# The first product of the second MLP in seven half products a pair of tiles, in place of eight

## The chip, the cores and the metric

The program runs on one core of a Trainium2 chip. The metric is the device time of one execution in microseconds (us). Before the change the median of three runs was 1889.66 us (1889.51 to 1891.02). The profile is of one execution; its span, from the first to the last instruction, is 1887.1 us.

## The reference, cut to what matters

The reference is one inference step of a two-layer diffusion backbone over 128 context tokens and 512 latent tokens, 640 in all, each of 1024 features. Each layer is a mixer (attention in layer 0, retention in layer 1) and an MLP of 4096 intermediate features with a squared ReLU:

```python
h = _rms(x, norm_mlp) * (1.0 + sc2) + sh2
x = x + g2 * (jnp.square(jax.nn.relu(h @ mlp_w1)) @ mlp_w2)
```

With h of 640 x 1024, `mlp_w1` of 1024 x 4096 and `mlp_w2` of 4096 x 1024, the two products of an MLP have the same number of multiplications. The change concerns `h @ mlp_w1` of layer 1, the last MLP before the final norm.

## The kernel before

Activations stand by feature: `xT` and the modulated input `ha` are tiles of 128 features x 640 tokens, and the 640 tokens are two halves of 320. Every number in a product is kept as a high part (fp32r, made by a cast on ScalarE, ACT) and a low part (what the cast left, made by a subtraction on VectorE, DVE). `mm` (L420 to L424) forms high x high, high x low and low x high: three matmuls for each contraction tile of 128 and each half of the tokens. In `ha` contraction tiles 0 to 7 are high parts and 8 to 15 low parts.

The MLP makes its 4096 intermediate features in 32 tiles of 128 (`w1(n)`), in four chunks of 8 tiles. A tile costs 8 contraction tiles x 2 halves x 3 = 48 matmuls of 128x320. `hidden` takes it out of PSUM: ReLU (L1217), square (L1218) and the cast (L841) on ACT, and the low part (L842) on DVE, into `g`. After each chunk 8 tiles of the second product (`w2`, also 48 matmuls each) read the chunk in `g`, and `residual` (L457, DVE) adds them to `xT`. For chunks 1 to 3 the first tile of the next chunk is multiplied before the `w2` tiles (`ahead`), and its ReLU comes after them.

Weights are streamed in one fixed order, `PLAN`: parts of 128x1024 numbers, two parts (1 MB) to a DMA into a buffer `wr`, of which there are two. `pump` prepares a part: the cast into `wh` (L180, ACT), and later, in `lows`, the subtraction into `wl` (L193, DVE). Four prepared parts are held (`SLOTS`); `done()` frees one after a tile and prepares the next. The instructions of each engine run in the order in which this code issues them. Sums of products stand in four PSUM tiles of two banks (`pp`), used in turn.

## Time and profile before

| | |
|---|---|
| median of three runs | 1889.66 us |
| profiled execution, span | 1887.1 us |
| PE (TensorE matmul) busy | 1825.5 us, 97% |
| DVE (VectorE) busy | 1074.8 us, 57% |
| ACT (ScalarE) busy | 782.0 us, 41% |
| POOL (GpSimd) busy | 185.0 us, 10% |
| HBM traffic | 94 GB/s over the span |

Only the medians and spans are given: of the profiled execution no other time than its span is known, so 2.56 us stand between it and the median. The second MLP runs from about 1413 us to the end. "Busy" of PE is from modelled ends of pipelined matmuls, so how close PE is to its rate is read from the starts of its matmuls. In a row of the timeline the first column is the start in us from the span's start, the second the duration in us; in brackets stands the idle time before it and who ended it.

### The profile page before, as it was taken

To read this page: it belongs to the slowest core of one execution; us is meant where nothing else is said; L and a number is where in the kernel's file an instruction comes from. 1 tells how busy PE (TensorE), PEld (TensorE's weight loads), DVE (VectorE), ACT (ScalarE), POOL (GpSimd) and SP (SyncE) were. 2 spreads that over 40 slices of the span, in tenths; PEclk is the share of its full clock that TensorE was granted. 3 is DMA by queue.
4 is the path that set the end of the run, shared out by engine and by line. 5 is a ranking of instruction groups with operands and counts; after the bars stand their busy time and mean duration, and the time that the engine had idled before them with its cause. 6 is when DMAs were issued, how large, how long until landed. Compare 5 with 4: busy or idle time off the path is not lost.

```text
span 1887.1 us, 28520 instructions
## 1 busy us (share of the span) xinstructions
PE 1825.5 (97%) x11844; PEld 1715.8 (91%) x11844; DVE 1074.8 (57%) x1855; ACT 782.0 (41%) x1288; POOL 185.0 (10%) x242
## 2 busy tenths in 40 slices
PE   6998899999999999999999999999999999999997
PEld 4885688999999999998898898899899999999997
DVE  5767887668778663466645645555556332323235
ACT  5546776561322413266324324324347224142332
POOL 0124754200000000030000000000011000000002
PEclk9999999999999999999999999999999999999999
DMA  8205201135544432222122122112112222122111
GB/s 325 95 26 201 90 23 33 58 143 197 196 157 167 149 133 67 68 79 68 66 90 67 68 86 71 68 67 71 65 66 85 73 69 88 67 72 86 68 67 57
DMA packets 44481, 179.01 MB, mean 95 GB/s; under 512 B 3232, under 2 KB 5536, under 8 KB 40768
## 3 DMA queue, kind: packets, MB, share of 16 engines
q1 hardware_dynamic: 42624, 171.81, 26.3%
q0 software_dynamic: 1728, 5.38, 0.8%
q8 instruction: 93, 1.52, 0.3%
q14 instruction: 36, 0.29, 0.0%
HBM read 170.10 MB, written 7.08 MB: 94 GB/s over the span
## 4 chain that ended last, share of the span: by engine, by line
PE 89%; DVE 6%; ACT 2%; issue 1%; POOL 1%; DMA 0%; SPq 0%; POOLq 0%; DVEq 0%; ACTq 0%
PE pp L420 25%; PE pp L422 25%; PE pp L424 25%; PE pp L1433 2%; PE pp L1435 2%; PE pp L1434 2%; PE pt L891 1%; DVE ha L408 1%; PE s L837 1%; DVE xT L457 1%; PE s L838 1%; POOL p L1014 1%; PE x L260 1%; PE pv L898 1%; DVE tl L1029 1%
## 5 line engine op out<-in xcount | busy, mean ns | idle before, releaser
L180 ACT CAST wh<-wr 128x1024 fp32r<-128x1024 f32 x212 | 221.7, 1049 | 729.6 <-PE pp L422 706.5
L422 PE MATMUL pp<-ha,wh 128*128 128x320 f32 x1728 | 410.6, 310 | 7.3 <-DVE ha L408 7.2
L420 PE MATMUL pp<-ha,wh 128*128 128x320 f32 x1728 | 415.4, 312 | 0.0
L424 PE MATMUL pp<-ha,wl 128*128 128x320 f32 x1728 | 409.4, 309 | 1.7 <-DVE wl L193 1.7
L422 PEld LDWEIGHTS pp<-ha,wh 128*128 128x128 f32 x1728 | 292.8, 188 | 11.3 <-DVE ha L408 11.1
L420 PEld LDWEIGHTS pp<-ha,wh 128*128 128x128 f32 x1728 | 292.6, 188 | 8.0 <-issue 5.6
L424 PEld LDWEIGHTS pp<-ha,wl 128*128 128x128 f32 x1728 | 292.8, 188 | 2.3 <-DVE wl L193 2.0
L193 DVE TENSOR_TENSOR wl<-wr,wh 128x1024 fp32r<-128x1024 f32 x212 | 258.1, 1219 | 34.1 <-ACT wh L180 33.2
L457 DVE SCALAR_TENSOR_TENSOR xT<-pp,mod,xT 128x128 f32<-128x128 f32 (+1 forms) x360 | 135.6, 433 | 229.3 <-PE pp L424 229.3
L420 PE MATMUL pp<-g,wh 128*128 128x320 f32 x1024 | 245.4, 310 | 0.0
L422 PE MATMUL pp<-g,wh 128*128 128x320 f32 x1024 | 243.3, 308 | 0.0
L424 PE MATMUL pp<-g,wl 128*128 128x320 f32 x1024 | 243.3, 308 | 0.0
L420 PEld LDWEIGHTS pp<-g,wh 128*128 128x128 f32 x1024 | 173.2, 188 | 3.5 <-issue 3.3
L422 PEld LDWEIGHTS pp<-g,wh 128*128 128x128 f32 x1024 | 173.9, 188 | 0.2
L424 PEld LDWEIGHTS pp<-g,wl 128*128 128x128 f32 x1024 | 173.7, 188 | 0.0
L842 DVE TENSOR_TENSOR g<-s,g 128x640 fp32r<-128x640 f32 x64 | 52.8, 825 | 194.5 <-ACT g L841 194.5
L370 POOL TENSOR_TENSOR acc<-acc,sq 128x320 f32<-128x320 f32 x55 | 52.7, 959 | 995.8 <-ACT sq L366 993.5
L295 DVE SCALAR_TENSOR_TENSOR acc<-la,scond,acc 128x512 f32<-128x512 f32 x196 | 134.4, 746 | 0.0
L420 PE MATMUL pp<-qk,wh 128*128 128x320 f32 (+1 forms) x320 | 88.9, 326 | 0.0
L422 PE MATMUL pp<-qk,wh 128*128 128x320 f32 (+1 forms) x320 | 88.7, 326 | 0.0
L424 PE MATMUL pp<-qk,wl 128*128 128x320 f32 (+1 forms) x320 | 88.7, 325 | 0.0
L1014 POOL TENSOR_TENSOR p<-p,den 128x640 f32<-128x640 f32 (+2 forms) x64 | 70.0, 1095 | 51.2 <-DVE den L1007 25.7
(277 smaller groups left out, 2542.8 us busy)
## 6 DMA issues: line engine op xcount, KB each, us to landing
wr<-in_w SPq DMA_DIRECT2D x121, 1024.0 KB, 4.9
la<-in_wl SPq DMA_DIRECT2D x28, 1024.0 KB, 4.8
raw<-in_w SPq DMA_DIRECT2D x8, 1024.0 KB, 15.8
out_st<-o POOLq DMA_DIRECT2D x16, 256.0 KB, 2.6
xT<-in_x SPq DMA_DIRECT2D x4, 640.0 KB, 6.0
out_y<-xT SPq DMA_DIRECT2D x6, 320.0 KB, 2.3
wr<-in_w SPq DMA_DIRECT2D x2, 512.0 KB, 16.3
con<-in_con SPq DMA_DIRECT2D x1, 640.0 KB, 16.8
```

Source lines behind the costliest of these rows:

```text
L180: nc.scalar.copy(hi, r)
L193: self.nc.vector.tensor_tensor(lo, r, hi.bitcast(F32), ALU.subtract)
L295: nc.vector.scalar_tensor_tensor(a, w, s, a, ALU.mult, ALU.add)
L370: nc.gpsimd.tensor_tensor(acc, acc, sq[:, :HALF], ALU.add)
L420: mm(out[i], wh, rh[i], start=start, stop=False)
L422: mm(out[i], wh, rl[i], start=False, stop=False)
L424: mm(out[i], wl, rh[i], start=False, stop=stop)
L457: self.nc.vector.scalar_tensor_tensor(x, ps[:, s - o:e - o], g[:, k:k + 1], x, ALU.mult, ALU.add)
L842: self.nc.vector.tensor_tensor(lo, src, hi.bitcast(F32), ALU.subtract)
L1014: nc.gpsimd.tensor_tensor(p, p, d.to_broadcast(p.shape), ALU.mult)
L1433: mm(out, self.ha[:, kt, q], hi[:, c], start=kt == 0, stop=False)
L1434: mm(out, self.ha[:, kt, q], lo[:, c], start=False, stop=False)
```

## The change

`PAIRED = (1,)` sends the MLP of layer 1 to `mlp_paired`. Tiles 0 to 7 are made as before. Tiles 8 to 31 are made as 12 pairs by `pair_products`, four pairs in each of three chunks. For a pair the weights are four quarters of 128x512, q0 and q1 (the first tile's two halves of the contraction), q2 and q3 (the second tile's), all in one buffer `wr`. The input is four quarters H(i,j), with token half i and contraction half j. A product of a weight quarter and an input quarter is 4 contraction tiles x 3 = 12 matmuls of 128x320. There are seven, named here by the part of the weights and the form of the input:

- a/11 = q0 H(0,0) and a/12 = q1 H(0,1); c/1 = (q2-q0) S1; c/3 = (q3-q2) S3; d/2 = (q3-q2+q0) S2; d/22 = (q1-(q3-q2+q0)) H(1,1); b/4 = q3 S4
- S1 = H(1,0)+H(1,1), S2 = S1-H(0,0), S3 = H(0,0)-H(1,0), S4 = H(0,1)-S2

Three PSUM tiles take them: `a` gathers a/11, d/2, c/3 and d/22 one after the other, `b` c/1 and b/4, `cc` a/12. Between, ACT copies `a` out three times (into x0, y0, y1), and DVE adds `cc` and `b`. `forms` makes the S in 8 steps, beside tiles 5 to 7 and the first five `w2` tiles; S3 takes the place of H(1,0) in `ha`. `sums_ahead` and `more_sums` make the sums of the weights, the second in place in `wr`. The parts a, c and d of a pair use the four slots; b has a room of its own (`ph`, `pl`, one buffer each), is prepared by `last_part`, and only then is `wr` given back for the next DMA. `old` holds a pair's last steps and runs in the next pair, behind its d/2. The tile made `ahead` is gone. The diff, without its hunks that only take out comments:

```diff
     def mlp(l):
         m = [("w1", l, n) for n in range(8)]
+        if l in PAIRED:
+            for c in range(3):
+                m += [("w2", l, c, n) for n in range(8)]
+                m += [("w1", l, 8 * (c + 1) + n) for n in range(8)]
+            return m + [("w2o", l, r, n) for r in (6, 7) for n in range(4)]
         for c in range(4):
...
     def fill(self):
-        done = self.pos - bool(self.low) - self.pending
+        done = self.behind[0][0] if self.behind else self.pos - bool(self.low) - self.pending
         while self.dma_at < self.most and self.dma_at < (done // 2 + RAWS) * 2:
...
                 return
+            elif paired(what):
+                if self.held >= SLOTS:
+                    return
+                self.pair_part(raw, what)
             else:
                 if self.held >= SLOTS:
...
+    def sums_ahead(self):
+        if self.sub == 0 and self.sums is None and paired(PLAN[self.pos]):
+            q = self.raws[self.pos // 2].rearrange("p (q n) -> p q n", q=4)
+            self.sums = self.pairs.tile([P, SUB + SUB // 4], F32, tag="sums", name="sums")
+            t = self.sums[:, :SUB].rearrange("p (q n) -> p q n", q=2)
+            self.nc.vector.tensor_tensor(t, q[:, 2:4], q[:, 0:3:2], ALU.subtract)
+    def more_sums(self):
+        if self.sub == 1 and not self.summed:
+            self.lows()
+            q = self.raws[self.pos // 2].rearrange("p (q n) -> p q n", q=4)
+            t = self.sums[:, SUB // 2:SUB]
+            self.nc.vector.tensor_tensor(q[:, 0], t, q[:, 0], ALU.add)
+            self.nc.vector.tensor_tensor(q[:, 1], q[:, 1], q[:, 0], ALU.subtract)
+            self.summed = True
+    def pair_part(self, raw, what):
+        k = self.sub
+        if k == 0:
+            self.sums_ahead()
+        elif k == 1:
+            self.more_sums()
+        hi = self.wsp.tile([P, SUB], F32R, tag="wh", name="wh")
+        lo = self.wsp.tile([P, SUB], F32R, tag="wl", name="wl")
+        self.held += 1
+        src = self.sums[:, :SUB] if k == 1 else raw[:, :SUB]
+        self.nc.scalar.copy(hi, src)
+        self.lows()
+        self.low = (lo, src, hi)
+        self.parts[what[1], what[2] // 2, "acd"[k]] = hi, lo
+        self.sub = (k + 1) % 3
+        if k == 1:
+            self.summed = False
+        if k == 2:
+            self.sums = None
+            self.behind.append((self.pos, (what[1], what[2] // 2, "b"), raw))
+            self.pos += 2
+    def last_part(self):
+        self.lows()
+        i, key, raw = self.behind.pop(0)
+        hi = self.pairs.tile([P, SUB // 2], F32R, tag="ph", name="ph")
+        lo = self.pairs.tile([P, SUB // 2], F32R, tag="pl", name="pl")
+        src = raw[:, 3 * SUB // 2:]
+        self.nc.scalar.copy(hi, src)
+        self.nc.vector.tensor_tensor(lo, src, hi.bitcast(F32), ALU.subtract)
+        self.parts[key] = hi, lo
+        self.fill()
+    def part(self, *what):
+        while what not in self.parts:
+            self.pump()
+        return self.parts[what]
...
+    def forms(self, sf):
+        nc = self.nc
+        tt = nc.vector.tensor_tensor
+        def quarter(i, j, lo, k):
+            kt = 8 * lo + 4 * j + k
+            return self.ha[:, kt:kt + 2, HALF * i:HALF * i + HALF].bitcast(F32)
+        def split(hi, lo, t):
+            nc.scalar.copy(hi, t)
+            tt(lo, t, hi.bitcast(F32), ALU.subtract)
+        for k in (0, 2):
+            a, b = (self.tmp.tile([P, NT], F32, tag="t", name=n).rearrange("p (k n) -> p k n", k=2) for n in "ab")
+            out = [[sf[:, f, i, k:k + 2] for i in range(2)] for f in range(3)]
+            tt(a, quarter(1, 0, 0, k), quarter(1, 1, 0, k), ALU.add)
+            tt(b, quarter(1, 0, 1, k), quarter(1, 1, 1, k), ALU.add)
+            tt(a, a, b, ALU.add)
+            split(*out[0], a)
+            yield
+            tt(a, a, quarter(0, 0, 0, k), ALU.subtract)
+            tt(a, a, quarter(0, 0, 1, k), ALU.subtract)
+            split(*out[1], a)
+            yield
+            tt(a, quarter(0, 1, 0, k), a, ALU.subtract)
+            tt(a, a, quarter(0, 1, 1, k), ALU.add)
+            split(*out[2], a)
+            yield
+            tt(a, quarter(0, 0, 0, k), quarter(1, 0, 0, k), ALU.subtract)
+            tt(b, quarter(0, 0, 1, k), quarter(1, 0, 1, k), ALU.subtract)
+            tt(a, a, b, ALU.add)
+            split(*(self.ha[:, k + 8 * i:k + 2 + 8 * i, HALF:] for i in range(2)), a)
+            yield
+    def pair_products(self, l, c, sf, g):
+        nc = self.nc
+        st = {}
+        def form(f):
+            if f in ("1", "2", "4"):
+                return [sf[:, "124".index(f), i] for i in range(2)]
+            i, j = {"11": (0, 0), "12": (0, 1), "22": (1, 1), "3": (1, 0)}[f]
+            return [self.ha[:, 8 * o + 4 * j:8 * o + 4 * j + 4, HALF * i:HALF * i + HALF] for o in range(2)]
+        def product(p, w, half, f, out, start, stop, ks=range(4)):
+            hi, lo = self.part(l, p, w)
+            ah, al = form(f)
+            for k in ks:
+                s = slice(512 * half + P * k, 512 * half + P * k + P)
+                self.mm([out], hi[:, s], lo[:, s], [ah[:, k]], [al[:, k]], start and k == 0, stop and k == ks[-1],
+                        more=not start)
+        def begin(p):
+            a = self.pp()[:, :HALF]
+            x, y = (self.tmp.tile([P, NT], F32, tag="t", name=n) for n in "xy")
+            st[p] = a, x, y
+            product(p, "a", 0, "11", a, True, True)
+            nc.scalar.copy(x[:, :HALF], a)
+        def free():
+            self.held -= 1
+        first = 4 * (c + 1)
+        self.last_part()
+        old = None
+        for p in range(first, first + 4):
+            end = p == first + 3
+            if p == first:
+                begin(p)
+            a, x, y = st.pop(p)
+            b = self.pp()[:, :HALF]
+            x0, x1, y0, y1 = (t[:, HALF * i:HALF * i + HALF] for t in (x, y) for i in range(2))
+            product(p, "c", 0, "1", b, True, True)
+            product(p, "d", 0, "2", a, False, True)
+            if old:
+                old()
+            self.more_sums()
+            nc.scalar.copy(y0, a)
+            cc = self.pp()[:, :HALF]
+            product(p, "a", 1, "12", cc, True, True, range(2) if end else range(4))
+            if not end:
+                free()
+                nc.vector.tensor_tensor(x0, cc, x0, ALU.add)
+                self.pump()
+                nc.scalar.activation(x0, x0, ACTF.Relu)
+                self.lows()
+            product(p, "c", 1, "3", a, False, True)
+            free()
+            nc.scalar.copy(y1, a)
+            nc.vector.tensor_tensor(y1, b, y1, ALU.add)
+            self.pump()
+            self.lows()
+            if end:
+                product(p, "a", 1, "12", cc, False, True, range(2, 4))
+                free()
+                nc.vector.tensor_tensor(x0, cc, x0, ALU.add)
+                nc.scalar.activation(x0, x0, ACTF.Relu)
+                self.pump()
+                self.lows()
+            else:
+                begin(p + 1)
+                self.sums_ahead()
+            product(p, "d", 1, "22", a, False, True)
+            free()
+            nc.scalar.activation(x1, a, ACTF.Relu)
+            if not end:
+                self.pump()
+            nc.scalar.activation(x, x, ACTF.Square)
+            product(p, "b", 0, "4", b, False, True)
+            def old(p=p, x=x, y=y, b=b, y0=y0, end=end):
+                n = 2 * (p - first)
+                nc.vector.tensor_tensor(y0, b, y0, ALU.add)
+                if end:
+                    self.split(g[:, n], g[:, KT + n], x)
+                nc.scalar.activation(y, y, ACTF.Relu)
+                self.lows()
+                if not end:
+                    self.last_part()
+                    self.split(g[:, n], g[:, KT + n], x)
+                nc.scalar.activation(y, y, ACTF.Square)
+                self.split(g[:, n + 1], g[:, KT + n + 1], y)
+        old()
+        self.pump()
+    def mlp_paired(self, l, second):
+        nc = self.nc
+        mp, close = self.scope(f"mlp{l}")
+        g = mp.tile([P, 16, NT], F32R, name="g")
+        sf = mp.tile([P, 3, 2, 4, HALF], F32R, name="sf")
+        self.pairs = mp
+        g2 = self.modc(l, 5)
...
+        self.first_group([("w1", l, n) for n in range(4)], self.ha, second, hidden, scratch())
+        forms = self.forms(sf)
+        for n in range(4, 8):
+            ps = self.pp()
+            self.gemm_in(ps, *self.take("w1", l, n), self.ha)
+            self.done()
+            hidden(n, ps)
+            if n > 4:
+                next(forms)
+        for c in range(4):
+            if c:
+                self.pair_products(l, c - 1, sf, g)
+            if c == 3:
+                break
+            for n in range(8):
+                ps = self.pp()
+                self.gemm_in(ps, *self.take("w2", l, c, n), g)
+                self.done()
+                self.residual_both(n, ps, g2)
+                next(forms, None)
...
     def mlp(self, l, second):
+        if l in PAIRED:
+            return self.mlp_paired(l, second)
         nc = self.nc
```

The order of PE's instructions shows the same work before and now. First a tile of the first product before (buffer numbers are kept; `ha` is the input, `wh` and `wl` the weights' parts):

```order
L420 MATMUL pp_14893<-ha_3896,wh_14705 128x320 [waits Activation_49]
L420 MATMUL pp_14893<-ha_3896,wh_14705 128x320
L422 MATMUL pp_14893<-ha_3896,wh_14705 128x320 x2
L424 MATMUL pp_14893<-ha_3896,wl_14706 128x320 [waits DVE_49]
L424 MATMUL pp_14893<-ha_3896,wl_14706 128x320
L420 MATMUL pp_14893<-ha_3896,wh_14705 128x320 x2
L422 MATMUL pp_14893<-ha_3896,wh_14705 128x320 x2
```

Now the first rows of five products in a row of the second pair of the second paired chunk: d/2 and a/12, c/3 into the PSUM tile of d/2 (pp_15498, `a`), a/11 of the next pair, d/22 again into pp_15498:

```order
L501 MATMUL pp_15498<-sf_13430,wh_15494 128x320 [waits Activation_49]
...
L501 MATMUL pp_15587<-ha_3896,wh_15404 128x320 [waits Activation_49]
...
L501 MATMUL pp_15498<-ha_3896,wh_15475 128x320 [waits Activation_49]
...
L501 MATMUL pp_15624<-ha_3896,wh_15529 128x320 [waits DVE_49]
...
L501 MATMUL pp_15498<-ha_3896,wh_15494 128x320 [waits Activation_49]
...
L501 MATMUL pp_15545<-sf_13430,ph_15573 128x320 [waits DVE_49]
```

A tile has given way to products of 12 matmuls over one half of the tokens, and c/3, d/22 and b/4 wait for an engine that reads or adds up the sum before them.

ACT's order before, for two tiles of the first product in a row:

```order
L180 CAST wh<-wr 128x1024 [waits PE_49]
L1217 ACTIVATE r<-pp 128x640 [waits PE_49]
L1218 ACTIVATE s<-r 128x640 [waits DVE_49,Activation_49]
L841 CAST g<-s 128x640 [waits Activation_49]
L180 CAST wh<-wr 128x1024 [waits DMAHW2_49,PE_49]
L1217 ACTIVATE r<-pp 128x640 [waits PE_49]
L1218 ACTIVATE s<-r 128x640 [waits DVE_49,Activation_49]
L841 CAST g<-s 128x640 [waits Activation_49]
```

ACT's order now, for that pair, from the ReLU of the pair before (L1403, first row of `old`) on; an L241 and the square L1395 follow:

```order
L1403 ACTIVATE y<-y 128x640 [waits DVE_49]
L260 CAST ph<-wr 128x512 [waits PE_49]
L926 CAST g<-x 128x640 [waits Activation_49]
L1408 ACTIVATE y<-y 128x640 [waits Activation_49]
L926 CAST g<-y 128x640 [waits Activation_49]
L1365 COPY y<-pp 128x320 [waits PE_49]
L241 CAST wh<-sums 128x1024 [waits PE_49]
L1372 ACTIVATE x<-x 128x320 [waits DVE_49]
L1376 COPY y<-pp 128x320 [waits PE_49]
L241 CAST wh<-wr 128x1024
L1345 COPY x<-pp 128x320 [waits PE_49]
L1392 ACTIVATE x<-pp 128x320 [waits PE_49]
```

ACT has 14 instructions for a pair in place of 8, and the copy of `a` that c/3 waits for (L1365) stands behind five that finish the pair before.

## Rows read from the trace of the kernel before

**Rows 1.** From the page: busy time of each engine, the clock granted to PE in 40 slices, and the chain that ended last, by engine and line.

```profile
PE 1825.5 (97%) x11844; PEld 1715.8 (91%) x11844; DVE 1074.8 (57%) x1855; ACT 782.0 (41%) x1288; POOL 185.0 (10%) x242
...
PEclk9999999999999999999999999999999999999999
...
PE 89%; DVE 6%; ACT 2%; issue 1%; POOL 1%; DMA 0%; SPq 0%; POOLq 0%; DVEq 0%; ACTq 0%
```

**Rows 2.** Busy time by stretch: the stretch and its length, busy us (and instructions) of each engine, PE's granted clock, DMA share, GB/s.

```profile
1500.00:1800.00 300.00, 300.00 (x2048) 300.00 (x2047) 90.57 (x132) 88.64 (x106) 0.00 (x0) 1.00 0.22 75
...
1857.00:1887.00 30.00, 19.33 (x125) 18.18 (x123) 18.40 (x38) 6.78 (x15) 9.35 (x11) 0.86 0.25 88
```

**Rows 3.** The same view of a short stretch at the start of the second MLP, where PE waits several times.

```profile
1420.00:1430.00 10.00, 7.58 (x45) 6.33 (x44) 8.41 (x15) 8.68 (x20) 3.82 (x4) 1.00 0.19 77
```

**Rows 4.** All that PE waited for from 1400 us to the end: us in total, times, the longest.

```profile
PE pp L422 <- DVE ha L408: 2.4, 3, 1.2
PE pp L382 <- POOL acc L370: 1.2, 1, 1.2
```

**Rows 5.** The timeline across tiles of the second product, in order of time.

```profile
1508.04 1.05 ACT L180 CAST wh<-wr 128x1024 fp32r<-128x1024 f32 x1 [5.98 <-PE pp L422]
1508.13 0.46 PE L420 MATMUL pp<-g,wh 128*128 128x320 f32 x2
...
1508.33 1.14 DVE L457 SCALAR_TENSOR_TENSOR xT<-pp,mod,xT 128x128 f32<-128x128 f32 x3 [4.77 <-PE pp L424]
...
1515.17 0.46 PE L420 MATMUL pp<-g,wh 128*128 128x320 f32 x2
...
1515.37 1.14 DVE L457 SCALAR_TENSOR_TENSOR xT<-pp,mod,xT 128x128 f32<-128x128 f32 x3 [4.77 <-PE pp L424]
```

**Rows 6.** PE's timeline in `first_group`, whose products are over one half of the tokens at a time into one PSUM tile.

```profile
1432.01 0.31 PE L420 MATMUL pp<-ha,wh 128*128 128x320 f32 x1
1432.16 0.31 PE L422 MATMUL pp<-ha,wh 128*128 128x320 f32 x1
1432.30 0.31 PE L424 MATMUL pp<-ha,wl 128*128 128x320 f32 x1
...
1440.81 0.31 PE L420 MATMUL pp<-ha,wh 128*128 128x320 f32 x1
```

**Rows 7.** Groups of instructions of the second MLP by line and shape: count, busy us, mean ns of one, idle time before.

```profile
L193 DVE TENSOR_TENSOR wl<-wr,wh 128x1024 fp32r<-128x1024 f32 x64 | 77.9, 1218 | 9.3 <-ACT wh L180 9.3
L180 ACT CAST wh<-wr 128x1024 fp32r<-128x1024 f32 x64 | 67.1, 1050 | 273.5 <-PE pp L422 273.5
L842 DVE TENSOR_TENSOR g<-s,g 128x640 fp32r<-128x640 f32 x32 | 26.4, 826 | 138.3 <-ACT g L841 138.3
L457 DVE SCALAR_TENSOR_TENSOR xT<-pp,mod,xT 128x320 f32<-128x320 f32 x48 | 25.5, 542 | 0.9 <-PE pp L424 0.9
L1218 ACT ACTIVATE s<-r 128x640 f32<-128x640 f32 x32 | 23.7, 739 | 1.0
L841 ACT CAST g<-s 128x640 fp32r<-128x640 f32 x32 | 23.3, 728 | 1.0
...
L400 DVE TENSOR_TENSOR o<-xT,rstd 128x320 f32<-128x320 f32 x8 | 5.8, 738 | 0.0
...
L400 DVE TENSOR_TENSOR scr<-xT,rstd 128x320 f32<-128x320 f32 x8 | 3.7, 486 | 0.0
L406 ACT CAST ha<-scr 128x320 fp32r<-128x320 f32 x8 | 3.7, 461 | 0.3
...
L375 ACT ACTIVATE rstd<-pp,eps 128x320 f32<-128x320 f32 x3 | 1.6, 528 | 3.9 <-PE pp L382 2.5 <-PE pp L384 1.4
```

**Rows 8.** The same view of the whole run, for widths that the second MLP does not have.

```profile
L1391 DVE TENSOR_TENSOR r<-r,sw 128x512 f32<-128x512 f32 x16 | 11.1, 692 | 0.6
...
L1139 ACT CAST wh<-wr 128x512 fp32r<-128x512 f32 x16 | 10.1, 629 | 1.5 <-PE x L422 1.5
```

**Rows 9.** ACT's timeline over two tiles of the first product in a row.

```profile
1445.34 0.70 ACT L1217 ACTIVATE r<-pp 128x640 f32<-128x640 f32 x1
1446.07 0.74 ACT L1218 ACTIVATE s<-r 128x640 f32<-128x640 f32 x1
1446.84 0.73 ACT L841 CAST g<-s 128x640 fp32r<-128x640 f32 x1
1447.47 1.05 ACT L180 CAST wh<-wr 128x1024 fp32r<-128x1024 f32 x1
```

**Rows 10.** The timeline around one of PE's waits in Rows 4.

```profile
1427.32 0.64 DVE L408 TENSOR_TENSOR ha<-o,ha 128x320 fp32r<-128x320 f32 x1 [0.45 <-ACT ha L406]
...
1427.78 0.31 PE L420 MATMUL pp<-ha,wh 128*128 128x320 f32 x1
1428.02 0.41 PE L422 MATMUL pp<-ha,wh 128*128 128x320 f32 x1
...
1428.27 0.31 PE L424 MATMUL pp<-ha,wl 128*128 128x320 f32 x1
```

**Rows 11.** The weights' DMAs between 1500 and 1800 us: count, KB each, median us from issue to landing.

```profile
wr<-in_w SPq DMA_DIRECT2D x21, 1024.0 KB, 4.9
```

More of the change, by code (lines that the diff above doesn't have):

```diff
@@ L42 @@
 RATES, MOST = (1.278, 0.926, 0.798), 2.076
+PAIRED = (1,)
 ENDS = (0, 2, 4, 6, 7)
@@ L59, with paired @@
 RC, NRC = columns(("row", 896), ("cosr", 8), ("sinr", 8), ("cosc", 64), ("sinc", 64))
+def paired(part):
+    return part[0] == "w1" and part[1] in PAIRED and part[2] >= 8
 def plan():
@@ L100, in plan @@
     for i, s in enumerate(out):
+        if paired(s):
+            assert i % 2 == s[2] % 2
         if s[0] == "ada":
@@ L139, in __init__ @@
         self.low = None
+        self.sub = 0
+        self.parts = {}
+        self.sums = None
+        self.summed = False
+        self.behind = []
         self.pending = 0
@@ L186, in pump @@
             n -= 1
+    def sums_ahead(self):
[28 more added lines that the diff above has]
+        if k == 1:
+            self.summed = False
+        if k == 2:
+            self.sums = None
+            self.behind.append((self.pos, (what[1], what[2] // 2, "b"), raw))
[14 more added lines that the diff above has]
+        return self.parts[what]
     def lows(self):
@@ L411, in modulate, with mm @@
                 yield
-    def mm(self, out, wh, wl, rh, rl, start, stop):
-        mm = self.nc.tensor.matmul
+    def mm(self, out, wh, wl, rh, rl, start, stop, more=False):
+        def mm(*a, **k):
+            return self.nc.tensor.matmul(*a, **k, skip_group_check=more)
         n = range(len(out))
@@ new lines, in mlp_paired, with scratch, hidden @@
+    def mlp_paired(self, l, second):
[5 more added lines that the diff above has]
+        g2 = self.modc(l, 5)
+        def scratch():
+            t = mp.tile([P, SUB + SUB // 4], F32, tag="sums", name="scr")
+            return [t[:, HALF * i:HALF * i + HALF] for i in range(4)]
+        def hidden(n, ps):
+            s = self.tmp.tile([P, NT], F32, tag="t", name="s")
+            nc.scalar.activation(self.two(s), self.both(ps), ACTF.Relu)
+            nc.scalar.activation(s, s, ACTF.Square)
+            self.split(g[:, n], g[:, KT + n], s)
+        self.first_group([("w1", l, n) for n in range(4)], self.ha, second, hidden, scratch())
[18 more added lines that the diff above has]
+                next(forms, None)
+        for n in range(4):
+            hi, lo = self.take("w2o", l, 6, n)
+            for m in range(2):
+                ps = self.pp()
+                self.gemm([ps[:, :HALF], ps[:, 512:512 + HALF]], (0, 1), hi, lo, lambda j: 256 * j + 128 * m,
+                          g, range(4), KT)
+                if m:
+                    self.done()
+                self.residual_both(2 * n + m, ps, g2)
+        self.ending = True
+        second = self.last_piece([("w2o", l, 7, n) for n in range(4)], g, range(4, 8), KT, g2, self.final, scratch())
+        close()
+        return second
```

## The prediction

> **What bounds the kernel now.** I read the page first [rows 1]: PE is busy 97% of the span, its clock stands at full in every slice, and 89% of the chain that ended last is PE. Busy ends of matmuls are modelled, so I looked next at the stretch that the change touches. From 1500 to 1800 us PE is busy without a gap, DVE for 90.6 of 300 us, ACT for 88.6, POOL not at all, and the clock is 1.00, which is 2.4 GHz [rows 2]. The list of waits says the same from the other side: from 1400 us to the end PE waited 3.6 us in all, at the norm that opens the MLP and at the one that ends it [rows 4]. So inside the second MLP nothing but the number of matmuls sets the time, and the price of one is the distance between starts. A tile of 48 starts at 1508.13 and the next at 1515.17 us: 7.04 us, or 146.7 ns a matmul, waits at the border included [rows 5]. The new products run over one half of the tokens into one PSUM tile; so does `first_group`, and there 60 matmuls lie between the starts at 1432.01 and 1440.81 us: again 146.7 ns [rows 6]. The pace does not depend on which half or whose turn it is.
>
> **What goes.** A pair took 2 x 48 = 96 matmuls, now 7 x 12 = 84. Twelve pairs: 144 fewer x 0.1467 us = 21.1 us. A pair then lasts 84 x 0.1467 = 12.32 us on PE in place of 14.08, a single product 1.76. The trace has no idle time that this could come from, so it is all on the path, unless something else now makes PE wait.
>
> A rule of the Trainium skill would price it lower ("VectorE: DVE Perf Modes", section "The TRN2 errata"): a matmul takes its columns plus six cycles at 2.4 GHz. For 320 columns that is 135.8 ns by estimate, 19.6 us for 144, and a run of 1870.7 us; the rows' 146.7 ns decide.
>
> **What is added, engine by engine.** DVE for a pair: three low parts of 1024 at 1.22, sums of 1024 at 1.22, two sums of 512 at 0.69 and a low part of 512 at 0.69, three additions of 320 with one operand in PSUM at 0.54, two low parts of 640 at 0.83 [rows 7, 8]: 10.2 us. ACT: three casts of 1024 at 1.05, one of 512 at 0.63, two of 640 at 0.73, three instructions of 640 at 0.74, and five of 320 (SBUF 0.46, out of PSUM 0.53; I take 0.5): 10.0 us [rows 7, 8]. Both fit under 12.32, at 83 and 81%, where two tiles kept DVE for 2 x (1.22 + 0.83) = 4.1 us and ACT for 2 x (1.05 + 0.70 + 0.74 + 0.73) = 6.4 in 14.08 [rows 7, 9]. So the question is order, not sum.
>
> I lay one pair out from t = 0, where PE starts c/1. PE: c/1 to 1.76, d/2 to 3.52, a/12 to 5.28, c/3 to 7.04, the next a/11 to 8.80, d/22 to 10.56, b/4 to 12.32. A sum in PSUM can be read 0.20 us after the next product starts (matmul 1508.13, DVE 1508.33 [rows 5]). Of instructions in a row on ACT, one that reads the last one's result starts 0.03 us after its end, any other 0.10 us before it [rows 9].
>
> - The tightest hand-over is c/3, which adds into `a` and waits for the copy of `a` (L1365). Before that copy ACT has five instructions of `old`. DVE's addition of b runs from 0.20 to 0.74; ReLU to 1.51, cast of `ph` from 1.41 to 2.04, cast of x from 1.94, square from 2.57, cast of y from 3.33, copy from 3.96 to 4.46. c/3 starts at 5.28: 0.8 us to spare. Were none of these overlapped, the copy would end at 4.9 and still be in time.
> - In the last pair of a chunk only half of a/12 stands before c/3, which starts at 4.40. There the copy is 0.06 to 0.5 us late. A wait costs PE more than its length: DVE ended at 1427.96, the waiting matmul started at 1428.02 and the next 0.25 after it, not 0.147, so 0.16 us on top [rows 10]. Three chunks at 0.2 (near the overlapped case, which rows 9 show): 0.6 us; bounds 0 and 3 x 0.66 = 2.0.
> - d/22 waits for the copy of `a` after c/3: ready at 7.24, ACT frees itself at about 7.2 (cast of c waits for a/12's end, 5.5 to 6.5, then the ReLU of x0), copied by 7.8, wanted at 8.80. b/4 wants y1 + b: 8.3 against 10.56. The next c/1 wants the PSUM tile that the ReLU of x1 frees: 11.3 against 12.32. The parts c and d of the next pair are ready at 7.9 and 10.0, wanted at 12.32 and 14.08.
> - DMA: the buffer comes free when `last_part` has its low part, at about 2.7; 4.9 us to land [rows 11] gives 7.6, and DVE asks for it at 9.8. Nothing else is queued on SP there. SP's and POOL's instructions are as many as before.
>
> `forms` adds 28 instructions of 640 on DVE and 8 on ACT, once, 4 x 0.83 = 3.3 us of DVE at most beside a tile of 7.04 that keeps it for 1.22 + 1.14 [rows 5, 7]: covered, and first read three tiles after its last step. The tile `ahead` covered the last ReLU of a chunk; now the first `w2` tile reads that tile only in its last eighth, 6.16 us after it starts. From that start its chain is 0.2 until PSUM can be read, ACT's cast for the next weights, ReLU, square and cast, and the low part on DVE [rows 7, 9]: 0.20 + 1.05 - 0.10 + 0.70 + 0.74 + 0.73 + 0.83 and three steps of 0.03 are 4.2 us, covered. If that cover were gone it would cost 2 us once a chunk. After a pair the chain is ReLU, square, cast, low part from 0.74 on: 3.9 us against 6.16.
>
> One thing the trace does not show: a product that goes on adding to a PSUM tile which ACT has just read. Four products of a pair do so (d/2, c/3, d/22, b/4), 48 in all. Bounds: nothing, as for the waits met in time at tile borders, where the pace holds [rows 5]; or a wake of 0.16 us each, 7.7 us in all [rows 10]. I take nothing, because it is the nearer row: those waits too are for engines that have long been done.
>
> **The sum.** 1887.1 - 21.1 + 0.6 = 1866.6 us of span. The median stands 2.56 us above the span, so 1869.2 us.
>
> **Rivals.**
> - Hand-overs cost a wake each (the open point above): 1869.2 + 7.7 = 1876.9. For it: PE, which had one waiting point a tile, has one in six of seven products. Against: each is met with 0.8 us or more to spare.
> - DVE becomes the bound, and the kernel slower. At 10.2 us it decides from 12.32 on, a factor 1.2, and eats the whole gain at 14.08, a factor 1.38. The trace has such a factor: the same product of 320 takes 0.738 us beside POOL and 0.486 without it [rows 7], 1.52. Then a pair takes 15.5 us, 12 x 1.4 = 17 more than before: 1907. Against: POOL has no instruction between 1500 and 1800 us [rows 2], and none is added.
> - PE's clock falls in the paired stretch because of short idle times. In 1857 to 1887 us, where PE is busy 19.3 of 30, the granted clock is 0.86 [rows 2]. At that the 148 us of pairs would take 172, 24 more: 1893, slower. Against: with 2.4 us idle in 10 the clock stayed at 1.00 [rows 3]. The Trainium skill has a rule to this effect ("TensorE: Matmul & The Clock Gate", section "A second HAM failure mode: psum-queue depth-cycling"): products that cycle through PSUM banks with short pauses let the clock swing between its levels; by rows 3 it doesn't here.
> - That the change doesn't do what it says is ruled out by the order: 144 matmuls fewer on PE, and the same shape.
>
> **Chances.** My forecast 0.68 (own range 1867.5 to 1871, from no wait at all, with the runs' spread of 1, to 2.0 us of waits); wakes 0.23; DVE 0.05; clock 0.04. The range runs from 1867.0 to 1877.0: the forecast and most of the wakes, about 0.87. A difference of 0.2%, 3.8 us, is about what a measurement can tell from no change; the first two cases are faster by far more. DVE between the two factors gives some of the same. Faster 0.91, same 0.03, slower 0.06.
>
> **What would show it.** Right: in the new profile PE's starts in the paired stretch are 146.7 ns apart throughout, a pair takes 12.3 us, the waits of PE on ACT there come to about half a microsecond in all, at c/3 in the last pair of a chunk, and DVE and ACT are near 80% busy. Wrong: waits of PE on ACT or DVE at d/22 or b/4 in every pair (wakes, or an order that I read too kindly), DVE busy without gaps, a clock below 1.00, or ACT standing at its third cast of a pair for a DMA.

## The result, and the profile after

The changed kernel takes 1867.8 us, the median of four runs (1866.57 to 1868.63), beside 1889.59 us of the kernel before, measured together with it (four runs, 1889.0 to 1891.02). The ratio is 0.9884, with a 95% interval from 0.987 to 0.9898: 21.8 us or 1.2% faster. The forecast was 1869.2. The profiled execution took 1866.57 us, with a span of 1864.8.

From the page of the changed kernel, the lines that answer to [rows 1]:

```profile
PE 1804.8 (97%) x11700; PEld 1694.9 (91%) x11700; DVE 1164.8 (62%) x1979; ACT 819.7 (44%) x1368; POOL 184.4 (10%) x242
...
PEclk9999999999999999999999999999999999999999
...
PE 90%; DVE 5%; ACT 2%; DMA 1%; POOL 1%; issue 1%; POOLq 0%; SPq 0%; DVEq 0%; ACTq 0%
```

PE has 144 matmuls fewer and is busy 20.7 us less; DVE has taken on 90 us and ACT 38. The share of PE in the span (97%) and in the chain (89, now 90%) has hardly moved: the kernel is bound as before, by fewer matmuls.

Stretches as in [rows 2], with PE, PEld (PE's weight loads), DVE, ACT and POOL busy in turn, then the granted clock. The first holds the pairs with the `w2` tiles between them, but for the last products of the twelfth pair; the second is as long as one pair:

```profile
1500.00:1790.00 290.00, 290.00 (x1978) 289.77 (x1977) 166.82 (x234) 124.19 (x182) 0.00 (x0) 1.00 0.23 78
...
1549.63:1561.95 12.32, 12.32 (x86) 12.32 (x85) 9.57 (x13) 8.90 (x14) 0.00 (x0) 1.00 0.25 85
```

Between 1500 and 1790 us PE has no gap and the full clock, 2.4 GHz. All that PE waited for from 1395 us on, which answers to [rows 4] (lines have other numbers now: L501 is the matmul of L420 to L424, L464 that of L382):

```profile
PE pp L501 <- DVE ha L490: 2.4, 3, 1.2
PE pp L464 <- POOL acc L452: 1.1, 1, 1.1
```

They are the two norms' waits, as before. Of the pairs not one wait is listed. PE's timeline shows where a pair begins, and the one kind of place where it stumbles:

```profile
1561.23 0.46 PE L501 MATMUL pp<-sf,wh 128*128 128x320 f32 x2
...
1573.55 0.46 PE L501 MATMUL pp<-sf,wh 128*128 128x320 f32 x2
...
1577.51 0.46 PE L501 MATMUL pp<-ha,wh 128*128 128x320 f32 x2
1577.81 0.31 PE L501 MATMUL pp<-ha,wl 128*128 128x320 f32 x1
1577.95 0.54 PE L501 MATMUL pp<-ha,wh 128*128 128x320 f32 x2
1578.32 0.31 PE L501 MATMUL pp<-ha,wl 128*128 128x320 f32 x1
```

From c/1 of one pair to c/1 of the next are 12.32 us, 146.7 ns a matmul, the pace of [rows 5, 6]. The second of these pairs is a chunk's last. Its c/3 begins at 1577.95, on pace; from there two matmuls take 0.37 us to the next row's start, where two in a row take 0.29 everywhere else. ACT's copy for it ended at 1577.87:

```profile
1577.45 0.42 ACT L1365 COPY y<-pp 128x320 f32<-128x320 f32 x1
```

That is the late hand-over of the forecast: it just does not hold c/3 up, and costs 0.08 us behind its first matmul. The same 0.08 stands at c/3 of the other two chunk ends (1683.63 and 1789.31) and at no other product.

ACT's timeline over the pair before, whose c/1 begins at 1561.23 (the first of its five instructions ahead of the copy waits for DVE's addition L1400):

```profile
1561.95 0.74 ACT L1403 ACTIVATE y<-y 128x640 f32<-128x640 f32 x1 [0.28 <-DVE y L1400]
1562.60 0.60 ACT L260 CAST ph<-wr 128x512 fp32r<-128x512 f32 x1
1563.11 0.72 ACT L926 CAST g<-x 128x640 fp32r<-128x640 f32 x1
1563.73 0.73 ACT L1408 ACTIVATE y<-y 128x640 f32<-128x640 f32 x1
1564.50 0.73 ACT L926 CAST g<-y 128x640 fp32r<-128x640 f32 x1
1565.13 0.42 ACT L1365 COPY y<-pp 128x320 f32<-128x320 f32 x1
1566.56 1.05 ACT L241 CAST wh<-sums 128x1024 fp32r<-128x1024 f32 x1 [1.00 <-PE pp L501]
```

The copy that c/3 waits for (L1365) ends at 1565.55, 4.32 us into the pair; c/3 is due at 5.28. So 0.96 us are to spare, where the forecast had 0.8. After it ACT stands idle for 1.00 us until a/12 has ended: these idle times behind the hand-overs are what the order has in reserve.

Groups of instructions of the second MLP by line and shape, which answer to [rows 7, 8] (mean ns of one behind the busy time):

```profile
L218 DVE TENSOR_TENSOR sums<-wr 128x1024 f32<-128x1024 f32 x12 | 14.6, 1220 | 0.0
...
L226 DVE TENSOR_TENSOR wr<-sums,wr 128x512 f32<-128x512 f32 x12 | 8.3, 688 | 0.1
L260 ACT CAST ph<-wr 128x512 fp32r<-128x512 f32 x12 | 7.3, 605 | 0.0
...
L1400 DVE TENSOR_TENSOR y<-pp,y 128x320 f32<-128x320 f32 x12 | 5.9, 489 | 17.0 <-PE pp L501 17.0
...
L1365 ACT COPY y<-pp 128x320 f32<-128x320 f32 x12 | 5.1, 421 | 9.3 <-PE pp L501 9.3
...
L1372 ACT ACTIVATE x<-x 128x320 f32<-128x320 f32 x9 | 4.2, 470 | 1.4 <-DVE x L1370 1.4
```

The widths known from elsewhere in the kernel held (1.22, 0.69, and 0.60 where I took 0.63). The two kinds that had to be taken from a neighbouring row came out shorter: an addition out of PSUM 0.49 (I took 0.54), a copy out of PSUM 0.42 to 0.44 (I took 0.5).

### The profile page after: what moved, and what is told of

The parts are those of the page before. It is cut to its first block, busy times and chain, and to the rows that moved or that the text cites. A ratio compares the mean times of both kernels' runs of the same rounds, so it can differ in the third digit from the quotient of the medians.

```text
span 1864.8 us, 28407 instructions
## 1 busy us (share of the span) xinstructions
PE 1804.8 (97%) x11700; PEld 1694.9 (91%) x11700; DVE 1164.8 (62%) x1979; ACT 819.7 (44%) x1368; POOL 184.4 (10%) x242
## 4 chain that ended last, share of the span: by engine, by line
PE 90%; DVE 5%; ACT 2%; DMA 1%; POOL 1%; issue 1%; POOLq 0%; SPq 0%; DVEq 0%; ACTq 0%
PE pp L501 76%; PE pp L1703 2%; PE pp L1705 2%; PE pp L1704 2%; PE x L501 1%; DMA raw<-in_w 1%; PE pt L976 1%; POOL p L1099 1%; DVE ha L490 1%; DVE xT L542 1%; PE s L922 1%; PE s L923 1%; PE x L342 1%; DVE tl L1114 1%; PE pv L983 1%
## 5 line engine op out<-in xcount | busy, mean ns | idle before, releaser
L501 PE MATMUL pp<-ha,wh 128*128 128x320 f32 x3072 | 612.4, 312 | 7.3 <-DVE ha L490 7.2
L501 PEld LDWEIGHTS pp<-ha,wh 128*128 128x128 f32 x3072 | 491.6, 188 | 19.8 <-DVE ha L490 11.0
L501 PE MATMUL pp<-g,wh 128*128 128x320 f32 x2048 | 393.7, 310 | 0.0
L501 PE MATMUL pp<-ha,wl 128*128 128x320 f32 x1536 | 381.7, 309 | 0.0
L501 PEld LDWEIGHTS pp<-g,wh 128*128 128x128 f32 x2048 | 323.5, 188 | 3.6 <-issue 3.3
L501 PEld LDWEIGHTS pp<-ha,wl 128*128 128x128 f32 x1536 | 265.2, 188 | 0.6 <-DVE wl L275 0.3
L501 PE MATMUL pp<-g,wl 128*128 128x320 f32 x1024 | 243.5, 309 | 0.0
L501 PEld LDWEIGHTS pp<-g,wl 128*128 128x128 f32 x1024 | 173.8, 188 | 0.0
L501 PE MATMUL pp<-qk,wh 128*128 128x320 f32 (+1 forms) x640 | 140.5, 326 | 0.0
L377 DVE SCALAR_TENSOR_TENSOR acc<-la,scond,acc 128x512 f32<-128x512 f32 x196 | 134.5, 748 | 0.0
L501 PEld LDWEIGHTS pp<-qk,wh 128*128 128x128 f32 x640 | 105.7, 188 | 5.7
L501 PE MATMUL pp<-qk,wl 128*128 128x320 f32 (+1 forms) x320 | 88.7, 325 | 0.0
L1703 PE MATMUL pp<-wh,ha 128*128 128x512 f32 x160 | 63.6, 397 | 0.0
L1705 PE MATMUL pp<-wh,ha 128*128 128x512 f32 x160 | 63.3, 395 | 0.0
L1704 PE MATMUL pp<-wl,ha 128*128 128x512 f32 x160 | 63.2, 395 | 0.0
L501 PEld LDWEIGHTS pp<-qk,wl 128*128 128x128 f32 x320 | 56.1, 188 | 2.9
```

Source lines behind the costliest of these rows:

```text
L377: nc.vector.scalar_tensor_tensor(a, w, s, a, ALU.mult, ALU.add)
L501: return self.nc.tensor.matmul(*a, **k, skip_group_check=more)
L1703: mm(out, self.ha[:, kt, q], hi[:, c], start=kt == 0, stop=False)
L1704: mm(out, self.ha[:, kt, q], lo[:, c], start=False, stop=False)
L1705: mm(out, self.ha[:, KT + kt, q], hi[:, c], start=False, stop=kt == KT - 1)
```

## The experiments

Each run had the kernel before on the same chip beside it; times are medians. "After" is 1867.8. It was measured apart from the runs below; differences taken from the ratios to the kernel before come out within 0.5 us of those given.

**Is it the count of matmuls?** One product of every pair is issued twice into the same PSUM tile (the second time it starts the sum anew), so a pair has eight half products in the new order:

```diff
+            product(p, "a", 0, "11", a, True, True)
             product(p, "a", 0, "11", a, True, True)
```

> The changed kernel, with the product a/11 of every pair made twice (the second time it starts its sum anew, so the outputs are the same): eight half products a pair, all the added work on DVE and ACT kept. If the time is the number of matmuls at 146.7 ns each, the 144 matmuls put back cost 21.1 us: 1867.8 + 21.1 = 1888.9, and PE still waits for nobody in the paired stretch. If part of the gain came from something else (the tile made ahead that is gone, the other order of the weights), it stays below 1887.5. If a wait had been hidden under the missing matmuls, less than 18 us come back.

Measured: 1890.01 us, ratio 1.0001 (0.9992 to 1.0011). PE's line of the page:

```profile
PE 1827.6 (97%) x11844; PEld 1717.3 (91%) x11844; DVE 1165.3 (62%) x1979; ACT 819.6 (43%) x1368; POOL 184.7 (10%) x242
```

11844 matmuls are exactly those of before, DVE and ACT still carry the new work, PE waits for nobody in the pairs, and the whole gain is gone. So the gain is the 144 matmuls, and the added 90 us of DVE and 38 of ACT cost nothing in pairs of 14.08 us. That they cost nothing in pairs of 12.32 either is read from the kernel after, where PE has no wait in the pairs but for the three slips of 0.08.

**Does the new order give or take anything by itself?** All 32 tiles plain, in the order of the changed kernel, without the tile made ahead:

```diff
 def paired(part):
-    return part[0] == "w1" and part[1] in PAIRED and part[2] >= 8
+    return False
...
-            if c:
-                self.pair_products(l, c - 1, sf, g)
+            for n in range(8) if c else ():
+                ...
+                hidden(n, ps)
```

> The changed kernel's order (no tile ahead of the second product, weights in the new order, hidden() in place) but all 32 tiles made plainly with 48 matmuls, no sums and no forms. By the number of matmuls the same as the kernel before: 1889.6 us within 1. If the order gives something by itself: lower by that, so that 21.8 us measured against 21.1 counted would be explained by some 0.7 us here. If the tile ahead had covered the last ReLU of a chunk after all: up to 6 us higher (2 us for each of three chunks).

Measured: 1889.01 us, ratio 0.9996 (0.9987 to 1.0006), and no wait of PE in the MLP but the norms' (3.6 us, as in [rows 4]). Dropping the tile ahead cost nothing, as the forecast had it.

**What does a hand-over cost that nothing covers, and what one that is covered?** In the nine pairs that have a successor, d/22 now follows c/3 at once, so PE must wait until ACT has copied c/3's sum:

```diff
-            else:
-                begin(p + 1)
-                self.sums_ahead()
             product(p, "d", 1, "22", a, False, True)
...
+            if not end:
+                begin(p + 1)
+                self.sums_ahead()
```

> The changed kernel with d/22 right behind c/3 and the next pair's a/11 behind d/22, in the nine pairs that are not the last of their chunk: the hand-over of the sum from PE to ACT and back has no product to cover it. As counted: 0.20 us until the sum can be read, 0.43 for the copy, about 0.06 until PE starts and 0.10 for its wake, 0.8 us a pair, 9 x 0.8 = 7.1: 1874.9 us, and the trace names ACT's copy L1376 as what PE waited for. If a sum that goes on where ACT has just read cost more than a plain wait (the open point of the prediction), more than 10 us; if hand-overs are free, 1867.8.

Measured: 1874.71 us, 6.9 more than after; ratio 0.9919 (0.9904 to 0.9934). PE's waits, and one of the nine in its timeline:

```profile
PE pp L501 <- ACT y L1376: 4.6, 9, 0.5
```

```profile
1558.15 0.56 PE L501 MATMUL pp<-ha,wh 128*128 128x320 f32 x2 [0.52 <-ACT y L1376]
```

Nine new waits and no other, each 0.52 us as listed. The list counts from the modelled end of the matmul before, 0.31 us after its start, and the next was due 0.15 after that start; and after the wait two matmuls take 0.40 us to the next row's start in place of 0.29. So a listed wait costs 0.16 + 0.11 = 0.27 us beyond its length: 0.79 here. Expected was 0.8 each, and 6.9 by 9 is 0.77. The other products that go on in a tile which another engine has just read (d/2 and c/3 behind ACT's copies, b/4 behind DVE's addition) show no wait here, nor do those of a pair in the kernel after: such a product costs something only when it comes too early.

**How much slack do the hand-overs have?** More work on ACT ahead of the copy that c/3 waits for, one copy or three of 128x640 into a tile that nobody reads, in nine pairs:

```diff
             if old:
                 old()
+                for _ in range(1):
+                    nc.scalar.copy(extra, self.xT[:, 0])
             self.more_sums()
             nc.scalar.copy(y0, a)
```

> In the nine pairs that finish an older pair inside them, ACT makes one more copy of 128x640 just ahead of the copy of L1365 that product c/3 waits for; it goes into a tile that nobody reads, so no work of the reference is left out. In the trace of the changed kernel such copies follow each other every 0.63 us, the copy of L1365 ends 4.32 us into an ordinary pair and c/3 begins at 5.28, so 0.96 us are to spare there, and in the last pair of a chunk c/3 begins 0.88 us sooner and already stands for 0.08. My theory (the hand-overs are covered by the order, and each has its own slack): six ordinary pairs cost nothing, the three at a chunk's end 0.63 each, 1.9 us in all: 1869.7, with PE waits on L1365 of 0.7 each, three times. Rival (ACT is nowhere in the way, the 0.08 is a start of its own): 1867.8 and no wait. Rival (ACT is near its limit, every delay goes through): 9 x 0.63 = 5.7, 1873.5.

Measured: 1868.89 us, ratio 0.9891 (0.9874 to 0.9907). The difference to after, 1.1 us, is too small to tell from none by itself; the waits tell it:

```profile
PE pp L501 <- ACT y L1368: 1.3, 3, 0.4
```

Three waits of 0.44, at the three chunk ends and nowhere else: six of nine hand-overs took 0.63 us more without a trace. With 0.27 beyond each wait the three come to 2.1 us, less the 0.2 of the slips that stood there before.

> As the run with one copy, with three of them: 1.89 us more ahead of the copy that c/3 waits for. My theory: in six ordinary pairs 1.89 - 0.96 = 0.93, and 0.16 for a start after a wait, 1.1 each, 6.5; in three pairs at a chunk's end 1.9 each, 5.7; 12.2 us in all: 1880, with nine PE waits on L1365. ACT is busy for 8.9 of a pair's 12.32 us, with the three copies for 10.8, so it keeps up otherwise. Rival (PE is held only where ACT as a whole runs out of time): 1867.8 to 1869. Rival (what ACT is late by is carried into the next hand-over too): 9 x 1.89 = 17 and more, 1885.

Measured: 1885.66 us, 17.9 more than after. PE's waits, and one of the six in ordinary pairs:

```profile
PE pp L501 <- ACT y L1368: 12.3, 9, 2.0
```

```profile
1570.25 0.56 PE L501 MATMUL pp<-ha,wh 128*128 128x320 f32 x2 [1.08 <-ACT y L1368]
```

Nine waits, 1.08 six times and 1.95 three times: with 0.27 each 14.7 us, where 12.2 were expected. The three copies set the hand-over back by 2.15 us and not by 1.89, as ACT's rows at that place show:

```profile
1567.63 2.24 ACT L1366 COPY extra<-xT 128x640 f32<-128x640 f32 x3
1569.78 0.42 ACT L1368 COPY y<-pp 128x320 f32<-128x320 f32 x1
```

The three, which write one tile, begin 0.76 us apart, and only the copy behind them comes after 0.63. By its sum ACT had room for them, 8.9 + 2.15 = 11.05 of 12.32 us. But 17.9 were paid. The rest shows in the clock behind the longer waits (stretch, length, PE, PEld, DVE, ACT and POOL busy, clock):

```profile
1570.30:1574.30 4.00, 4.00 (x27) 4.00 (x28) 2.31 (x4) 2.81 (x5) 0.00 (x0) 1.00 0.08 32
1583.90:1587.90 4.00, 3.99 (x18) 3.99 (x19) 0.49 (x1) 1.32 (x2) 0.00 (x0) 0.65 0.13 51
...
1696.00:1700.00 4.00, 4.00 (x27) 4.00 (x28) 1.04 (x2) 1.37 (x2) 0.00 (x0) 1.00 0.10 42
...
1806.50:1810.50 4.00, 4.00 (x17) 4.00 (x18) 0.30 (x1) 0.76 (x2) 0.00 (x0) 0.57 0.11 46
```

After a wait of 1.08 us PE starts 27 matmuls in 4 us, and as many after the wait of 1.95 that ended at 1695.98; after the other two of 1.95 only 17 or 18, the granted clock being at its lower level, 1.2 GHz, for most of these 4 us (0.65 and 0.57 on average). Ten matmuls too few are 1.5 us, twice 3: 17.7 in all.

**When does DVE become the bound?** Six additions more of 128x640 on DVE in nine pairs:

```diff
                 begin(p + 1)
                 self.sums_ahead()
+                for _ in range(6):
+                    nc.vector.tensor_tensor(extra, self.xT[:, 0], self.xT[:, 1], ALU.add)
             product(p, "d", 1, "22", a, False, True)
```

> DVE makes six more additions of 128x640 into a tile that nobody reads in each of nine pairs, behind the sums for the next pair; 0.74 us apart, 4.5 us a pair. No work of the reference is left out. DVE is busy for 9.6 us of an ordinary pair of 12.32 (8.4 in a pair in front of the last of a chunk), so it would have 14.1 (12.9) to do. My theory (DVE's work is free until it is more than a pair lasts, then the excess is paid, less what the buffers and the last pair of a chunk, with 6 us of work, take up): between 0 and 6 x 1.8 + 3 x 0.6 = 12.6 us, likeliest 6: 1874, with PE waits on DVE that the changed kernel has none of. Rival (DVE already sets the pace of the pairs in the changed kernel): 9 x 4.5 = 40 us, 1908. Rival (DVE is far from any limit): 1867.8, no waits.

Measured: 1898.66 us, 30.9 more than after and slower than before; ratio 1.005 (1.0033 to 1.0067). I had expected 6, and 12.6 at most. The chain is in the timelines of DVE, ACT and PE in turn:

```profile
1567.09 5.12 DVE L1392 TENSOR_TENSOR extra<-xT 128x640 f32<-128x640 f32 x6
1572.12 0.48 DVE L1403 TENSOR_TENSOR y<-pp,y 128x320 f32<-128x320 f32 x1
```

```profile
1572.64 0.74 ACT L1406 ACTIVATE y<-y 128x640 f32<-128x640 f32 x1 [4.23 <-DVE y L1403]
...
1575.81 0.42 ACT L1366 COPY y<-pp 128x320 f32<-128x320 f32 x1
```

```profile
1576.28 0.56 PE L501 MATMUL pp<-ha,wh 128*128 128x320 f32 x2 [2.89 <-ACT y L1366]
...
1577.30 0.74 PE L501 MATMUL pp<-ha,wh 128*128 128x320 f32 x2
...
1580.50 0.51 PE L501 MATMUL pp<-ha,wh 128*128 128x320 f32 x2
```

The six stand right ahead of the addition that begins `old`; ACT waits for that addition 4.23 us, has four more instructions before the copy, and c/3 waits 2.89 us for the copy. PE waited 20.1 us in nine such places. The idle time of DVE ahead of that addition in the kernel after, in an ordinary pair and at a chunk's end:

```profile
1561.43 0.49 DVE L1400 TENSOR_TENSOR y<-pp,y 128x320 f32<-128x320 f32 x1 [1.51 <-PE pp L501]
...
1573.75 0.49 DVE L1400 TENSOR_TENSOR y<-pp,y 128x320 f32<-128x320 f32 x1 [2.64 <-PE pp L501]
```

The six set the addition back by 5.03 us (1567.09 to 1572.12), not by the 4.5 of my expectation. Locally that is 5.0, less DVE's idle 1.5, less 0.96 of slack: 2.6 us in an ordinary pair; at a chunk's end it is 5.0 - 2.6 + 0.1 = 2.5. The nine waits come to 2.2 on average as listed, 2.4 with the 0.16 to the listed start. The sum over a pair is passed as well: 9.6 + 5.0 = 14.6 us of DVE in an ordinary pair, 8.4 + 5.0 = 13.5 in a chunk's last but one, 6 x 2.3 + 3 x 1.1 = 17 us above 12.32 in all. Between the additions at 1556.64 and 1572.12 DVE is idle for no more than 1.2 of 15.48 us. So DVE has become the bound here, and this run does not tell the slack from the sum. What my expectation had wrong is the length of the six, a relief by buffers that did not come (it put 6 us where its sum gave 12.6), and the price behind a wait. The row at 1577.30 shows that price: three matmuls take 0.80 us from there on (to 1578.10) in place of 0.44, until 1580.50. Falls like this followed five of the nine waits (the one of 2.89, both of 2.64, two of the three of 2.36) and none of those of 1.36 to 1.80. At 1.5 us each: 20.1 + 9 x 0.27 + 5 x 1.5 = 30.0 of the 30.9.

**Does the same change pay elsewhere?** The last eight tiles of the first MLP in four pairs as well, 48 matmuls fewer. There DVE also sums up modulations for later (L375, L377), which need the room of the S forms; all but the last were to end first, and the forms came in beside five `w2` tiles:

```diff
 def paired(part):
-    return part[0] == "w1" and part[1] in PAIRED and part[2] >= 8
+    return part[0] == "w1" and part[2] >= (8 if part[1] in PAIRED else 24)
...
+        w2(2, 0, 3)
+        for _ in self.side:
+            self.tail()
+        ...
+        w2(2, 3, 8, self.forms(sf))
+        self.pair_products(l, 2, sf, g)
```

> The changed kernel, and four more pairs: tiles 24 to 31 of the first MLP are made as pairs too, their forms beside the second product's tiles 3 to 7 of its third chunk; the last of the fourteen late modulations moves behind the pairs, to make room in SBUF. By the number of matmuls 4 x 12 x 0.1467 = 7.0 us less: 1860.8 us. The rival: DVE, which makes the late modulations beside that MLP, falls behind there with the forms, PE waits for weights or inputs, and 1 to 7 us of it are lost: 1862 to 1868.

Measured: 1878.3 us, ratio 0.9939 (0.9924 to 0.9954): 10.5 slower than after, not 7.0 faster. The list of PE's waits names it:

```profile
PE pp L501 <- ACT x L1345: 10.9, 1, 10.9
...
PE pp L501 <- DVE xT L542: 2.2, 1, 2.2
...
PE pp L403 <- ACT sum L397: 1.0, 2, 0.5
```

One wait of 10.9 us, for the copy of the first a/11. It stands on ACT behind casts of the forms, and these come at DVE's pace:

```profile
725.48 0.72 ACT L1295 CAST ha<-a 128x640 fp32r<-128x640 f32 x1 [5.59 <-DVE a L1316]
...
726.63 0.42 ACT L1345 COPY x<-pp 128x320 f32<-128x320 f32 x1
```

DVE was late because it began late: its queue held the forms only behind the fourth tile, while it stood idle in front of it:

```profile
676.13 0.17 DVE L408 TENSOR_TENSOR mod<-pp,vec 128x8 f32<-128x8 f32 x1 [5.82 <-PE pp L403]
...
684.60 1.13 DVE L542 SCALAR_TENSOR_TENSOR xT<-pp,mod,xT 128x128 f32<-128x128 f32 x3 [5.67 <-PE pp L501]
685.65 0.81 DVE L1301 TENSOR_TENSOR a<-ha 128x640 f32<-128x640 f32 x1
```

In the last 7 us of that wait and the 3 us behind it the clock was at its lower level, and so it was for a while behind the wait of 2.2, which ended at 794.53:

```profile
720.00:730.00 10.00, 2.90 (x11) 2.91 (x12) 9.14 (x13) 1.57 (x3) 0.00 (x0) 0.51 0.05 4
...
790.00:800.00 10.00, 7.82 (x43) 7.59 (x43) 10.00 (x19) 0.44 (x1) 0.00 (x0) 0.83 0.02 10
```

If the prices from the pairs hold here, the four waits cost 14.1 + 4 x 0.27, the two falls of the clock about 3: 18.2 us, less 7.0 of matmuls is 11.2. The four runs of this kernel lie within 5 us (1876.18 to 1881.23).

The second try is the same with other places: the forms from the third tile on, two a tile, each low part taken while the next form is added; the modulations at two steps a tile; the last one's loads asked for at once:

```diff
-        w2(2, 0, 3)
+        w2(2, 0, 2)
...
-        w2(2, 3, 8, self.forms(sf))
+        w2(2, 2, 8, self.forms(sf))
...
-                for _ in range(1 if n == 3 else 2):
+                for _ in range(2 if n < 5 else 1):
...
         self.side = self.ada_late(late, len(LATE) - 1, len(LATE))
+        next(self.side)
```

> A second try at making the last eight tiles of the first MLP in pairs too, beside the 24 of the second: 4 pairs x 12 x 0.1467 = 7.0 us fewer matmuls. The first try lost them, by its trace, at one place: PE stood 10.9 us for ACT's copy of L1345, which was queued on ACT behind the casts of the last of the eight sums of its input, and those were late because DVE began them only with the fourth tile of the group before (DVE was idle 13 us of the two tiles ahead of it); the clock fell to 0.51 there, and at 791 PE stood 2.2 us more behind a late load for the last modulation. Here the sums begin with the third tile and come two a tile, each sum's low half is taken while the next is added, the modulations run at two steps a tile so that they end before it, and the last one's loads are asked for as soon as the pairs leave their room. My theory (a pair gives 12 matmuls wherever its inputs are ready in time): 1867.8 - 7.0 = 1860.8, with up to 1 us back for single waits: 1860.8 to 1862. Rival (the sums of the input still come late, since DVE had 67 us of work in 100 there before): 1864 to 1872 with a PE wait on L1345 again. Rival (the added work collides elsewhere, in the modulations): PE waits on DVE at L542 or L403 of 5 us or more.

Measured: 1861.92 us (1861.29 to 1862.73, four runs), ratio to before 0.9855 (0.984 to 0.9869): faster than both kernels, 5.9 us less than after. (The kernel with one copy more on ACT, measured together with this one, took 1868.89.) The waits that are left in that MLP:

```profile
PE pp L502 <- DVE ha L491: 2.4, 3, 1.2
PE pp L404 <- ACT sum L398: 1.6, 3, 0.5
```

The first are the norm's, as ever; the second are the modulations that had to end before the room was free, three turns in a row that PE could not lay between other work. 7.0 of matmuls less 1.6 of waits leave 5.4, or 4.6 if 0.27 us go with each as in the pairs; 5.9 were measured, and the runs of either kernel differ by more than 1.3. So pairs pay in the first MLP too, and the first try failed by its order (where the forms, the modulations and the loads stand), not by the amount of DVE's work: that is the same in both tries (1209.4 and 1209.8 us busy).

## Why the prediction was right

**The saving, 144 x 0.1467 = 21.1.** Right. The pace in the pairs is 146.7 ns, and putting 144 matmuls back took the gain back (1890.0). The rule of the Trainium skill ("VectorE: DVE Perf Modes", section "The TRN2 errata") that the prediction weighed, 135.8 ns by estimate, does not agree: 84 matmuls of a pair would take 11.41 us by it, and the trace has 12.32. With the slips below the count gives 20.9; 21.8 is the difference of the medians, and the 0.9 between them is within what the runs of either kernel differ by (2.0 us).

**Late c/3 at a chunk's end, 0.2 each.** The place was right, the size was not: 0.08, by the PE row at 1577.95, and the copy was not late but 0.08 ahead of c/3's start, so that only the second matmul behind it slipped. The step that failed is the width of ACT's and DVE's work on PSUM, taken from [rows 7] with 0.5 and 0.54 where 0.42 to 0.44 and 0.49 came out; so the copy ends at 4.32 us into the pair and not 4.46, where c/3 of a chunk's end begins at 4.40. The sum lost 0.4 us by it. That a copy out of PSUM is shorter than one within SBUF (0.42 against 0.47 at L1372, same width) is what the Trainium skill has ("Perfetto Trace Analysis", section "Optimizing Scalar/DVE Operations": about 51 ns of overhead for ScalarE on PSUM, 93 on SBUF), and the trace agrees; I had it the other way round. The widths also made DVE and ACT look fuller, 10.2 and 10.0 us of a pair; from 1549.63 to 1561.95, just one pair, they are busy 9.6 and 8.9.

**Going on in a PSUM tile that ACT has just read, taken at nothing, bound 7.7.** Right: no wait in the pairs. The run with nine bare hand-overs shows that those which are early enough stay free while the nine cost 0.77 each. This rival, which had 0.23, is excluded: it would have put the kernel at 1876.9. (Of the four products that the prediction counts there, b/4 goes on in a tile that DVE has read and not ACT; it shows no wait either.)

**The cover of `forms` and of the dropped tile ahead, at nothing.** Right for this place; the plain kernel in the new order shows the second by itself. That the cover of `forms` is no property of the change was shown where it was missing: 10.9 us in the first MLP.

**DVE as the bound, 0.05.** It did not come about. Its factor of 1.52 was a mean of two lengths: of the eight additions with 0.738 us on average those that began while POOL was at work took 1.16 to 1.17 and the others 0.47 to 0.49; the pairs have no instruction of POOL beside them, and the same width took 0.49 there. Where DVE begins to decide is less sharp than the 12.32 us of the prediction: the slack in front of the next hand-over, about 2.5 us here (1.5 idle, 0.96 on ACT), is close to the room in its sum, 12.32 - 9.6 = 2.7, and the run with six additions passed both. For ACT the two lie apart, 0.96 and 3.4, and there the slack decided: three copies, 2.15 us, held c/3 up in all nine pairs.

**The clock, 0.04.** It did not fall, since PE never stood in the pairs. The argument of [rows 3] was too strong, though: "2.4 us idle in 10 and a clock of 1.00" is true of that stretch, and still a single wait of 1.95 us brought the clock down in another run. The rule that the prediction named from the Trainium skill ("TensorE: Matmul & The Clock Gate", section "A second HAM failure mode: psum-queue depth-cycling") speaks of short pauses between groups of products. The pairs cycle through three PSUM tiles without one, at a clock of 1.00 from 1500 to 1790 us, so the kernel after does not put it to the test; where the runs put pauses of 1.95 us and more into the pairs, the clock did swing, behind nine of 0.52 us it did not.

## What to carry to other kernels

Where one engine is busy without a gap, the saving is the number of its instructions by the distance between their starts, and everything else is a question of order: lay out one period for each in-order engine and write the slack at each hand-over beside it. Added work is free as long as it fits the slack in front of the next hand-over, not as long as the engine's busy sum fits the period (2.15 us on ACT, where the sum had 3.4 of room, cost 2.0 us each time). An engine that stands idle in front of work it could already do has that work too far back in its queue: begun a tile earlier and packed closer, with its loads asked for sooner, the same work turned 10.5 us lost into 5.9 gained.

## What the runs showed of the hardware

A wait of PE can cost more than its length, by the clock: of the nine waits of 1.08 to 1.80 us in the pairs none was followed by a lower granted clock, of three of 1.95 two were, of three of 2.36 two, and so were both of 2.64 and that of 2.89; in the first MLP the clock fell behind the wait of 2.18 and within that of 10.9. In the pairs the lower level then lasted about 3.5 us and cost about 1.5. Two waits of one length and at one place in the pair, 1.95 us ahead of 1583.91 and of 1696.0, differed in it; what decides was not tried and stays open.

At full clock a listed wait costs PE 0.27 us beyond its length (above), of which the prediction, from [rows 10], knew the part after the start. With that and the falls of the clock the times that four runs took above the kernel after come out within 1 us of the measured ones: 7.1 of 6.9, 1.9 of 1.1, 17.7 of 17.9 and 30.0 of 30.9.
